# Layer 1's MLP: token operands made in every run instead of kept in DRAM, and the norm's scale row in one piece

## The chip, the cores and the metric

The kernel runs on one core of a Trainium2 chip. The metric is the device time of one execution in microseconds (us). TensorE (PE, with its weight loads as PEld), VectorE (DVE), ScalarE (ACT), GpSimd (POOL) and SyncE (SP) each work through a queue of their own in order; DMAs are issued from the queues of SP and POOL. Three runs of the kernel before took 2901.81 to 2903.02 us, with a median of 2902.23 us.

## What is computed

One inference step of a two-layer decoder: 1024 prompt tokens and 8 sampled tokens go through gated linear attention, an MLP, differential attention with a paged cache, and a second MLP, each followed by a post-norm. The part at issue is the last one, the MLP of layer 1:

```python
def post_norm(x, f, g, b):
    return layer_norm(DEEPNORM_ALPHA * x + f, g, b)

def sq_relu_mlp(x, w1, w2):
    h = jax.nn.relu(x @ w1)
    return (h * h) @ w2
...
        x_p = post_norm(x_p, f_p, ln_mix_g[layer], ln_mix_b[layer])
        x_s = post_norm(x_s, f_s, ln_mix_g[layer], ln_mix_b[layer])
        x_p = post_norm(x_p, sq_relu_mlp(x_p, mlp_w1[layer], mlp_w2[layer]), ln_mlp_g[layer], ln_mlp_b[layer])
```

`w1` is 1024 x 4096, `w2` 4096 x 1024, everything float32.

## The kernel before

Each float32 product is made of three matmuls (`mm3`, lines 185 to 188): each operand is split into a rounded part `hi` (an ACT cast, L182 for tokens, L1415 for weights) and the rest `lo` (a subtraction: on DVE for tokens, L183, on POOL for weights, L1416), and PE adds hi·hi, hi·lo and lo·hi.

The MLP of layer 1 (`mlp1`) goes through the 4096 hidden columns in four groups, called g = 0 to 3 here; the change's title calls them runs. In each group it makes the hidden values from the tokens ("up") and multiplies them with `w2` ("down"). Both halves use a seven-product scheme for a 2 x 2 block matrix product in place of eight products. The tables `UP_W`, `UP_X`, `DOWN_H`, `DOWN_W` list for each product which quarters its two operands are made of; an operand with two terms is a difference or a sum of quarters, and "run" means that it goes on from the running quarter of the product before. For the tokens the running quarter is the tile `RX`, for the weights `RW`, and for the down results `RP` (128 x 4 x 512).

The up order is 1, 2, 5, 6, 4, 3, 7. An up product has 8 output tiles of 128 x 258 with 12 matmuls each; a down product has 4 output tiles of 128 x 512 with 12 matmuls each. Results are added on DVE into the hidden tile `HF` (L1458, L1459, or ACT copies L1461, L1465) or into the residual `Y` (L1489), and relu and square follow on ACT (L1447, L1448).

The tokens' operands are made by `chip_operand` into two buffers that take turns (XH.0 and XH.1; the profile names both XH, the queue rows XH_83 and XH_84). A buffer is free when the product before the current one has ended, so an operand is made while one product runs. For a two-term operand it does, for each of two halves: a DVE subtraction of two quarters (L1388, into `RX`), an ACT cast (L182) and a DVE subtraction (L183). For the up products this is done only in group 0. Then POOL's queue stores the two parts to the DRAM tile `xc` (L1393), and in groups 1 to 3 it loads them back (L1378, two loads of 1032 KB for each product) in place of making them. Down operands are made anew in every group. The source of the up operands, `xr(0)` and `xr(1)` (profile: XR), is not read again after group 0, so the last norm's two rows are loaded into it early (L1536).

Weight quarters are loaded on SP's queue (L1412); the second term of a sum is added by a DMA on POOL's queue (L1414). 

Post-norm needs the residual times ALPHA times the row `ln_mix_g`, plus ALPHA times the row `ln_mix_b`. `alpha_row` (lines 960 to 973) does this in four column pieces of 256: a DMA on SP's queue broadcasts a piece of the row into the tile `ht` (L965), and two DVE instructions of 128 x 4 x 256 apply it to tokens 0 to 3 and 4 to 7 (L970 for the scale, L972 for the shift). `ht` has one buffer (HTB = 1), so the next piece's DMA waits on SP's queue for the second DVE instruction of the piece before.

A scheduler that simulates the program sets each queue's order at build time, within the dependencies. `tc.issue_after` adds an order without a wait.

Of the kernel before, what the change touches and what calls it, by code (L numbers as in the profile page):

```python
# [12 lines left out]
F32R = mybir.dt.float32r  # L13
# [3 lines left out]
ALU = mybir.AluOpType  # L17
# [4 lines left out]
P = 128  # L22
D = 1024
# [8 lines left out]
ALPHA = 4.0 ** 0.25  # L32
# [72 lines left out]
UP_X = {1: [(0, 0)], 2: [(1, 0)], 5: [(0, 1), (0, 0)], 6: [(1, 1), "run"], 4: [(1, 0), "run"], 3: [(1, 1)], 7: [(0, 1), (1, 1)]}  # L105
# [5 lines left out]
def hybrid_step(ctx, tc, A, dbg=None, upto=9):  # L111
    nc = tc.nc
    V, S, G, TE = nc.vector, nc.scalar, nc.gpsimd, nc.tensor
    dma = nc.sync.dma_start
# [11 lines left out]
    def mmt():  # L126
        return mm.tile([P, 512], F32, name="mmt")

    def axt():
        return ax.tile([P, 512], F32, name="axt")  # L130
# [10 lines left out]
    dr = ctx.enter_context(tc.tile_pool(name="dr", bufs=1, space=DRAM))  # L141
# [9 lines left out]
    TH = 512 + NS // 2  # L151
# [3 lines left out]
    Yt = Y.rearrange("p (t n) -> p t n", n=D)  # L155
# [399 lines left out]
    for half in range(2):  # L555
        ps = smt()
        for k in range(NB):
            t = sload(w1[k * P : (k + 1) * P, half * 2048 : (half + 1) * 2048])
# [15 lines left out]
    for k in range(NB):  # L574
        t = sload(wd[k * P : (k + 1) * P, 0:2048])
# [13 lines left out]
    tmp = s2()[:, :128].rearrange("p (n d) -> p n d", d=16)  # L589
# [21 lines left out]
    for h in range(GH):  # L611
# [7 lines left out]
        for c in range(2):  # L619
# [4 lines left out]
            for i in range(4):  # L624
                a = slice(i * P, (i + 1) * P)
# [14 lines left out]
            for li, s in enumerate(LEVELS):  # L640
# [7 lines left out]
                for i in range(4):  # L648
                    for x in xs_:
                        y = 64 if s == 64 else x + TS  # L650
# [18 lines left out]
            for i in range(4):  # L669
                a = slice(i * P, (i + 1) * P)  # L670
# [5 lines left out]
            for i in range(4):  # L676
                a = slice(i * P, (i + 1) * P)
# [7 lines left out]
                t = 4 * c + i  # L685
# [8 lines left out]
    for h in range(GH):  # L694
        hi, lo = kunit(wi, 2048 + h * 256)
# [220 lines left out]
    steps_v, steps_g = [], []  # L916
# [43 lines left out]
    def alpha_row(v, op):  # L960

        for j in range(4):
            hs = slice(256 * j, 256 * j + 256)
            r = ht.tile([P, 256], F32, name="ht")
            dma(r, v[:, hs].broadcast_to([P, 256]))  # L965
            for t in (0, 4):
                y = Yt[:, t : t + 4, hs]
                rb = bc(r, [P, 4, 256], 1)
                if op == ALU.mult:
                    steps_v.append(V.scalar_tensor_tensor(y, y, ALPHA, rb, ALU.mult, ALU.mult).ins)  # L970
                else:
                    V.scalar_tensor_tensor(y, rb, ALPHA, y, ALU.mult, ALU.add)  # L972
            yield j
# [75 lines left out]
    for u in range(12):  # L1049
        hi, lo = kunit(wd, u * 256)  # L1050
        hv, lv = (x.rearrange("p (k n) -> p k n", n=256) for x in (hi, lo))
        for t2_ in range(4):
            ps = mmt()
            for i in range(2):
                t = 2 * t2_ + i
                a = slice(t * P, (t + 1) * P)
# [6 lines left out]
            if u < 8:  # L1063
                tmp = qt.tile([P, 2, 4, 16], F32, name="qr")
# [161 lines left out]
    for h in range(8):  # L1226
        head = nxt
        for n, t in enumerate((3, 2, 1, 0, 7, 6, 5, 4) if h == 7 else (7, 1, 5, 3, 6, 0, 4, 2)):
# [4 lines left out]
            at = t % 4 if h == 7 else t // 2  # L1233
# [34 lines left out]

    RP = hp.tile([P, 4, 512], F32, name="RP")

    XR = []

    def xr(c):
        if c == len(XR):
            XR.append(cp.tile([P, NB, TH], F32, name="XR%d" % c, tag="XL%d" % c))
        return XR[c]

# [88 lines left out]
    count = [0, 0]  # L1366
    loads = []

    def chip_operand(terms, quarter, n, tmp, kept=None):


        buf = XH.t[count[0] % 2].rearrange("p k n -> p (k n)")
        count[0] += 1
        parts = [buf[:, i * 4 * TH : i * 4 * TH + 4 * n] for i in range(2)]
        hi, lo = (x.rearrange("p (k n) -> p k n", n=n) for x in parts)
        if kept and kept[1]:
            for i in range(2):
                nc.gpsimd.dma_start(parts[i], kept[0][:, i])  # L1378
            return hi, lo
        rv, tv = (x[:, : 4 * n].rearrange("p (k n) -> p k n", n=n) for x in (RX, tmp))  # L1380
        for j in (0, 2):
            b = slice(j, j + 2)
            x = quarter(*terms[0])[:, b]
            if len(terms) > 1:

                y = rv[:, b] if terms[1] == "run" else quarter(*terms[1])[:, b]
                out = (tv if terms[1] != "run" else rv)[:, b]
                V.tensor_tensor(out, x, y, op=ALU.subtract)  # L1388
                x = out
            split(hi[:, b], lo[:, b], x)  # L1390
        if kept:
            for i in range(2):
                nc.gpsimd.dma_start(kept[0][:, i], parts[i])  # L1393
        return hi, lo

    def weight_operand(terms, quarter, side=None):
# [26 lines left out]

    w1, w2 = A["mlp_w1"][1], A["mlp_w2"][1]

    xc = dr.tile([7, P, 2, 4 * TH], F32R, name="xc")

    def operands(g, up, i):
        if up:
            left = weight_operand(UP_W[i], lambda h, k: (w1, 512 * k, 1024 * g + 512 * h))  # L1430
            right = chip_operand(UP_X[i], lambda k, c: xr(c)[:, 4 * k : 4 * k + 4, :], TH, RX, (xc[i - 1], g > 0))
            return left, right

        def beside(k, t):
            r, u = beside.quarter
            TE.matmul(acc[u][k * TS : (k + 1) * TS, :], hs[:, 4 * r + k, :], t, start=g == 0 and i in (1, 3), stop=g == 3 and r == 1)


        beside.quarter = ({1: (0, 0), 3: (1, 1), 7: (0, 1), 2: (1, 0)} if g < 3 else {1: (0, 0), 5: (0, 1), 6: (1, 0), 7: (1, 1)}).get(i)
        left = chip_operand(DOWN_H[i], lambda c, k: HF[:, 4 * k : 4 * k + 4, c, :512], 512, XF[0][:, : 4 * TH] if g == 3 and i == 7 else RX)  # L1440
        right = weight_operand(DOWN_W[i], lambda k, u: (w2, 1024 * g + 512 * k, 512 * u), beside if beside.quarter else None)
        return left, right
# [8 lines left out]
    def up_tile(g, i, m, c, left, right, ps):  # L1451
        (ah, al), (bh, bl) = left, right
        ps = ps[:, :CH]
        ms, cs = slice(m * P, (m + 1) * P), slice(c * CH, (c + 1) * CH)
        for k in range(4):
            mm3(ps, ah[:, k, ms], al[:, k, ms], bh[:, k, cs], bl[:, k, cs], k == 0, k == 3)
        c11, c12, c21, c22 = (HF[:, 4 * h + m, x, cs] for h in range(2) for x in range(2))
        add = lambda out, x, y: V.tensor_tensor(out, x, y, op=ALU.add)  # L1458
        less = lambda out, x, y: V.tensor_tensor(out, x, y, op=ALU.subtract)  # L1459
        if i == 1:  # L1460
            S.copy(c12, ps)  # L1461
        elif i == 2:
            add(c11, c12, ps)
        elif i == 5:
            S.copy(c22, ps)  # L1465
        elif i == 6:
            less(c21, ps, c12)
            add(c22, c22, c21)
        elif i == 4:
            add(c21, c21, ps)  # L1470
        elif i == 3:
            less(c12, ps, c22)
        else:
            add(c22, c22, ps)
            add(c21, c21, ps)
        if c:
            for h, x in {2: [(0, 0)], 3: [(0, 1)], 7: [(1, 1), (1, 0)]}.get(i, ()):
                hidden(h, x, m)
# [23 lines left out]
    def mlp1():  # L1502
        seq = []
        for g in range(4):
            seq += [(g, 1, i) for i in (1, 2, 5, 6, 4, 3, 7)]
            seq += [(g, 0, i) for i in ((1, 5, 6, 3, 7, 4, 2) if g < 3 else (1, 5, 6, 7, 4, 3, 2))]
        nxt = operands(*seq[0])
        n = 0
        for at, (g, up, i) in enumerate(seq):
            now = nxt  # L1510
            if not up and i == 1:
                if g == 0:
                    with tc.issue_after(steps_v[-1]):
                        list(alpha_row(A["ln_mix_g"][1:2], ALU.mult))
                    beta = alpha_row(A["ln_mix_b"][1:2], ALU.add)
                else:
                    for _ in range(2):
                        next(beta, None)
            for t in range(4):
                if t == 2 and at + 1 < len(seq):  # L1520
                    nxt = operands(*seq[at + 1])
                if up:
                    for c in range(2):
                        n += 1
                        up_tile(g, i, t, c, *now, axt() if n % 2 else mmt())
                    continue
                n += 1
                down_tile(g, i, t, *now, axt() if n % 2 else mmt())
                if g == 3:
                    for c, u in {7: [(1, 1)], 4: [(1, 0)], 3: [(0, 1)], 2: [(0, 0)]}.get(i, ()):  # L1530
                        yield 4 * c + t, u
            if g == 3 and not up and i == 7:
                samples_out()
            if g == 3 and up and i == 7:
                for x, nm in ((fg, "g"), (fb, "b")):
                    dma(x, A["ln_mlp_" + nm][1:2].broadcast_to([P, D]))  # L1536
                with tc.issue_after(loads[-1]):
                    for t0, t1 in ((0, 2), (4, 8)):
                        dma(A["y_prompt"][0, t0 * P : t1 * P], A["ln_mlp_b"][1:2].broadcast_to([(t1 - t0) * P, D]))
                spare.extend(XF[0][:, 4 * TH + 512 * j : 4 * TH + 512 * (j + 1)] for j in range(4))  # L1540
# [31 lines left out]
```

## Time and profile before

| | |
|---|---|
| median of three runs | 2902.23 us |
| the profiled execution's own time | 2897.76 us |
| its span in the profile | 2896.0 us |
| mean granted PE clock | 0.981 |
| MLP of layer 1, first up matmul to last down matmul | 2169.87 to 2877.17 us |
| DMA queue of SP: bytes | 520.66 MB |
| DMA queue of POOL: bytes | 112.50 MB |
| the DRAM tile `xc`: stores, loads | 14 and 42, 1032 KB each |

The busy share of an engine is a mean over stages. PE's matmuls overlap, so its busy time hides short gaps; waits are read from the list of waits, and a slower clock from the granted clock of a window. In the list of waits a row names the waiting engine and line, what ended the wait, the total in us, the count and the longest. In a window row the columns are the window, its length, and for PE, PEld, DVE, ACT and POOL the busy us and the number of instructions, then the granted PE clock, the DMA engines' busy share and GB/s.

### The profile page before, as it was taken

The page shows a single profiled execution, that of the slowest core. Times are in us where ns is not written, and L with a number is a line of the kernel's source. Part 1 is how long each engine was busy: PE and PEld are TensorE (multiplying, and loading weights), DVE is VectorE, ACT ScalarE, POOL GpSimd, SP SyncE. Part 2 cuts the span into 40 slices and gives each one's busy share as a digit, 9 for nine tenths or more (in the row PEclk, how much of TensorE's full clock was granted, in tenths as well). Part 3 has the DMA queues.
Part 4 walks back from the last instruction along what each step waited for, and adds up shares of the span by engine and source line. Part 5 has one row for each costly group of instructions (what it writes and reads, how often), then busy time and mean ns, then how long its engine had stood idle before and what let it go on. Part 6 is the DMA issues. An engine that isn't in the chain of part 4 may idle for free. (4 is left out here: it accounts for less than half of the span.)

```text
span 2896.0 us, 52075 instructions
## 1 busy us (share of the span) xinstructions
PE 2773.3 (96%) x19653; PEld 2267.4 (78%) x19653; DVE 1882.9 (65%) x2982; ACT 1043.5 (36%) x2075; POOL 1132.4 (39%) x867
## 2 busy tenths in 40 slices
PE   8889999999999999999999999989998999999997
PEld 5666767997777777777798988888988888797985
DVE  2565544567878777778768822888538846738378
ACT  3233444252221221221231112777424535345352
POOL 1231212234333433333333321122426766777664
PEclk9899999999999999999999998999999999999998
DMA  7557651624798898898668995463447678695894
GB/s 250 181 176 261 245 177 39 231 73 145 268 350 299 301 351 303 321 323 310 254 225 302 363 341 142 101 137 82 120 132 220 174 220 222 160 287 119 258 240 88
DMA packets 285366, 636.46 MB, mean 220 GB/s; under 512 B 25510, under 2 KB 141292, under 8 KB 273852
## 3 DMA queue, kind: packets, MB, share of 16 engines
q1 hardware_dynamic: 252716, 520.66, 52.4%
q0 software_dynamic: 32400, 112.50, 16.2%
q8 instruction: 154, 2.52, 0.4%
q14 instruction: 96, 0.79, 0.1%
HBM read 575.55 MB, written 44.06 MB: 214 GB/s over the span
## 5 line engine op out<-in xcount | busy, mean ns | idle before, releaser
L174 POOL TENSOR_TENSOR wlo<-raw,whi 128x512 fp32r<-128x512 f32 x256 | 357.1, 1408 | 730.1 <-ACT whi L173 635.8
L186 PE MATMUL mmt<-whi,XH 128*128 128x256 f32 (+1 forms) x1760 | 526.1, 300 | 2.2 <-ACT Y L310 2.0
L187 PE MATMUL mmt<-wlo,XH 128*128 128x256 f32 (+1 forms) x1760 | 525.9, 299 | 0.9 <-POOL wlo L174 0.9
L186 PE MATMUL mmt<-XH,whi 128*128 128x512 f32 (+1 forms) x1216 | 436.5, 360 | 7.0 <-DVE HL L183 6.6
L188 PE MATMUL mmt<-whi,XL 128*128 128x256 f32 x1536 | 436.6, 285 | 0.5 <-DVE XL L183 0.5
L188 PE MATMUL mmt<-XH,wlo 128*128 128x512 f32 (+1 forms) x1216 | 434.3, 358 | 0.0
L173 ACT CAST whi<-raw 128x512 fp32r<-128x512 f32 x256 | 153.1, 619 | 579.5 <-PE mmt L188 206.3
L187 PEld LDWEIGHTS mmt<-wlo,XH 128*128 128x128 f32 x1760 | 332.2, 189 | 30.9 <-issue 19.0
L186 PEld LDWEIGHTS mmt<-whi,XH 128*128 128x128 f32 x1760 | 331.5, 189 | 28.2 <-issue 13.5
L790 DVE TENSOR_REDUCE sc<-pg 128x16 f32<-128x1024 f32 x256 | 309.5, 1214 | 62.5 <-POOL pg L789 59.3
L187 PE MATMUL mmt<-XL,whi 128*128 128x512 f32 x768 | 307.3, 400 | 0.0
L188 PEld LDWEIGHTS mmt<-whi,XL 128*128 128x128 f32 x1536 | 289.8, 189 | 13.5 <-issue 11.8
L789 DVE TENSOR_TENSOR pg<-pg,qb 128x1024 f32<-128x1024 f32 x192 | 263.7, 1375 | 53.4 <-DMA pg<-in_cache_k 38.2
L789 POOL TENSOR_TENSOR pg<-pg,qb 128x1024 f32<-128x1024 f32 x64 | 158.8, 2482 | 297.9 <-DMA pg<-in_cache_k 182.4
L186 PEld LDWEIGHTS mmt<-XH,whi 128*128 128x128 f32 x1216 | 230.6, 190 | 54.8 <-issue 14.6
L188 PEld LDWEIGHTS mmt<-XH,wlo 128*128 128x128 f32 x1216 | 231.0, 190 | 38.1 <-issue 5.9
L187 PE MATMUL mmt<-wlo,HH 128*128 128x512 f32 x512 | 204.7, 400 | 0.0
L188 PE MATMUL mmt<-whi,HL 128*128 128x512 f32 x512 | 204.6, 400 | 0.0
L186 PE MATMUL mmt<-whi,HH 128*128 128x512 f32 x512 | 204.4, 399 | 0.0
L187 PEld LDWEIGHTS mmt<-XL,whi 128*128 128x128 f32 x768 | 145.5, 190 | 38.3 <-issue 7.1
L1416 POOL TENSOR_TENSOR wlo<-RW,whi 128x512 fp32r<-128x512 f32 x96 | 156.7, 1762 | 37.1 <-ACT whi L1415 37.1
L1416 POOL TENSOR_TENSOR wlo<-rw,whi 128x512 fp32r<-128x512 f32 x92 | 148.8, 1690 | 43.3 <-ACT whi L1415 43.2
(441 smaller groups left out, 5745.6 us busy)
## 6 DMA issues: line engine op xcount, KB each, us to landing
pg<-in_cache_k SPq DMA_DIRECT2D x256, 512.0 KB
pg<-in_cache_v SPq DMA_DIRECT2D x256, 512.0 KB
XH<-xc POOLq DMA_DIRECT2D x42, 1032.0 KB, 8.7
raw<-in_mlp_w SPq DMA_DIRECT2D x164, 256.0 KB
swt<-in_mlp_w SPq DMA_DIRECT2D x32, 1024.0 KB
rw<-in_mlp_w SPq DMA_DIRECT2D x116, 256.0 KB
RW<-in_mlp_w POOLq DMA_DIRECT2D x96, 256.0 KB, 6.1
xc<-XH POOLq DMA_DIRECT2D x14, 1032.0 KB, 7.6
```

Source lines behind the costliest of these rows:

```text
L173: S.copy(hi[:, c], raw)
L174: G.tensor_tensor(lo[:, c], raw, hi[:, c].bitcast(F32), op=ALU.subtract)
L186: TE.matmul(ps, ah, bh, start=first, stop=False)
L187: TE.matmul(ps, ah, bl, start=False, stop=False)
L188: TE.matmul(ps, al, bh, start=False, stop=last)
L789: eng.tensor_tensor(pg, pg, qb, op=ALU.mult)
L790: return V.tensor_reduce(sc[:, n, :], pg.rearrange("p (h d) -> p h d", d=64), op=ALU.add, axis=AX.X).ins
L1416: G.tensor_tensor(lo[:, k, :], t, hi[:, k, :].bitcast(F32), op=ALU.subtract)
```

## The change

Three edits, in one region.

1. `chip_operand` no longer has a kept form: the stores to `xc`, the loads from it and the tile itself are gone. All seven up operands are made in every group from `xr(0)` and `xr(1)`.
2. The whole scale row `ln_mix_g` is loaded once, by one DMA of 128 x 1024, into the first two of the four 512-column slices of `RP` before the MLP begins. `RP` is first written by the down products.
3. The scale is applied by eight DVE instructions of 128 x 1024, one token tile each, written in group 0 at the odd steps of the up products 5, 6, 4 and 3, in place of the four pieces at the first down product of group 0. The shift row keeps `alpha_row`.

```diff
     RP = hp.tile([P, 4, 512], F32, name="RP")
 
+    grow = RP[:, 0:2, :].rearrange("p a n -> p (a n)")
+    dma(grow, A["ln_mix_g"][1:2].broadcast_to([P, D]))
+
...
-    def chip_operand(terms, quarter, n, tmp, kept=None):
+    def chip_operand(terms, quarter, n, tmp):
...
-        if kept and kept[1]:
-            for i in range(2):
-                nc.gpsimd.dma_start(parts[i], kept[0][:, i])
-            return hi, lo
...
-        if kept:
-            for i in range(2):
-                nc.gpsimd.dma_start(kept[0][:, i], parts[i])
         return hi, lo
...
-    xc = dr.tile([7, P, 2, 4 * TH], F32R, name="xc")
-
...
-            right = chip_operand(UP_X[i], lambda k, c: xr(c)[:, 4 * k : 4 * k + 4, :], TH, RX, (xc[i - 1], g > 0))
+            right = chip_operand(UP_X[i], lambda k, c: xr(c)[:, 4 * k : 4 * k + 4, :], TH, RX)
...
                 if g == 0:
-                    with tc.issue_after(steps_v[-1]):
-                        list(alpha_row(A["ln_mix_g"][1:2], ALU.mult))
                     beta = alpha_row(A["ln_mix_b"][1:2], ALU.add)
...
+                    if g == 0 and 2 <= at < 6 and t % 2:
+                        y = Yt[:, 2 * (at - 2) + t // 2, :]
+                        steps_v.append(V.scalar_tensor_tensor(y, y, ALPHA, grow, ALU.mult, ALU.mult).ins)
```

The queue orders below are those of the built programs. Line numbers of the changed kernel differ: its scale step is L1520 (before: L970), its operand difference L1387 (L1388), its additions into the hidden tile L1452 (L1458), into the residual L1483 (L1489), its weight rest L1412 (L1416), its adding DMA L1410 (L1414); L183 and L972 are the same lines in both.

DVE in group 0's up products, before: from the second pair of scale steps on (a block of four stands a few rows ahead of it).

```order
L970 SCALAR_TENSOR_TENSOR Y<-Y,ht 128x4x256 x2
L1458 TENSOR_TENSOR HF<-HF,axt 128x258
L1388 TENSOR_TENSOR RX<-XR_25083,RX 128x1032
L1458 TENSOR_TENSOR HF<-HF,axt 128x258
L183 TENSOR_TENSOR XH_84<-RX,XH_84 128x1032
L1388 TENSOR_TENSOR RX<-XR_24816,RX 128x1032
L183 TENSOR_TENSOR XH_84<-RX,XH_84 128x1032
L970 SCALAR_TENSOR_TENSOR Y<-Y,ht 128x4x256 x2
L1388 TENSOR_TENSOR RX<-XR_24816,RX 128x1032
```

The same place in the changed kernel, from the difference for product 5 to that for product 6:

```order
L1387 TENSOR_TENSOR RX<-XR_25084,XR_24817 128x1032
L1520 SCALAR_TENSOR_TENSOR Y<-Y,RP 128x1024 x3
L953 TENSOR_SCALAR XR_25084<-axt,lnp 128x512
L1520 SCALAR_TENSOR_TENSOR Y<-Y,RP 128x1024
L183 TENSOR_TENSOR XH_83<-RX,XH_83 128x1032
L1452 TENSOR_TENSOR HF<-HF,axt 128x258
L1387 TENSOR_TENSOR RX<-XR_25084,RX 128x1032
L1452 TENSOR_TENSOR HF<-HF,axt 128x258
L183 TENSOR_TENSOR XH_83<-RX,XH_83 128x1032
```

Four of the eight scale steps stand ahead of the operand of product 5; the other four stand earlier still, beside the last tiles of the attention's output product; none is left among the operands that follow.

POOL in group 0's up products, before (`xc` rows are the stores of the operands):

```order
L1393 DMA xc<-XH_83 128x2064
L1414 DMA RW<-in_mlp_w 128x512
L1416 TENSOR_TENSOR wlo<-RW,whi 128x512 x2
L1393 DMA xc<-XH_84 128x2064
L1414 DMA RW<-in_mlp_w 128x512
L1393 DMA xc<-XH_84 128x2064
L1414 DMA RW<-in_mlp_w 128x512
L1416 TENSOR_TENSOR wlo<-RW,whi 128x512
L1416 TENSOR_TENSOR wlo<-rw,whi 128x512
```

And in the changed kernel:

```order
L1410 DMA RW<-in_mlp_w 128x512 x3
L1412 TENSOR_TENSOR wlo<-RW,whi 128x512
L1410 DMA RW<-in_mlp_w 128x512
L1412 TENSOR_TENSOR wlo<-RW,whi 128x512 x3
L1410 DMA RW<-in_mlp_w 128x512 x3
```

The weights' rests no longer stand behind a store that waits for a token operand.

DVE at the turn from group 1's down products to group 2's up products, before:

```order
L972 SCALAR_TENSOR_TENSOR Y<-ht,Y 128x4x256
L1489 TENSOR_TENSOR Y<-Y,mmt 128x512
L972 SCALAR_TENSOR_TENSOR Y<-ht,Y 128x4x256 x2
L1489 TENSOR_TENSOR Y<-Y,axt 128x512
L1489 TENSOR_TENSOR Y<-Y,mmt 128x512
```

And in the changed kernel:

```order
L972 SCALAR_TENSOR_TENSOR Y<-ht,Y 128x4x256
L1483 TENSOR_TENSOR Y<-Y,mmt 128x512
L972 SCALAR_TENSOR_TENSOR Y<-ht,Y 128x4x256 x2
L1483 TENSOR_TENSOR Y<-Y,axt 128x512
L183 TENSOR_TENSOR XH_83<-XR_24817,XH_83 128x1032
L1483 TENSOR_TENSOR Y<-Y,mmt 128x512
L183 TENSOR_TENSOR XH_83<-XR_24817,XH_83 128x1032
```

Group 2's first up operand now stands on DVE right behind the last two shift steps.

## The prediction

> **What bounds the kernel now.** I read the page's head first, then windows over the stages of the MLP, then PE's waits in them, then the timeline around the longest wait.
>
> ```profile
> span 2896.0 us, 52075 instructions
> PE 2773.3 (96%) x19653; PEld 2267.4 (78%) x19653; DVE 1882.9 (65%) x2982; ACT 1043.5 (36%) x2075; POOL 1132.4 (39%) x867
> ```
>
> PE is busy 96% of the span. The change removes no matmul, so it can gain only where PE waits or runs at a lower granted clock, and lose only where PE is made to wait anew. The windows of the four up stages (g = 0 to 3) and of one down stage:
>
> ```profile
> 2169.00:2263.00 94.00, 82.13 (x643) 80.14 (x642) 75.40 (x80) 45.44 (x81) 56.89 (x53) 0.93 0.78 228
> 2359.00:2441.00 82.00, 77.59 (x640) 76.05 (x638) 35.66 (x54) 37.12 (x79) 58.22 (x55) 1.00 0.91 265
> 2530.00:2612.00 82.00, 79.69 (x646) 77.33 (x647) 29.91 (x58) 36.16 (x74) 58.50 (x57) 1.00 0.92 271
> 2701.00:2783.00 82.00, 78.99 (x637) 77.08 (x636) 29.86 (x54) 36.22 (x78) 57.57 (x54) 0.98 0.96 276
> 2262.00:2345.00 83.00, 82.53 (x393) 62.77 (x392) 71.51 (x76) 42.79 (x76) 61.50 (x44) 1.00 0.61 145
> ```
>
> The same number of matmuls takes 94 us in group 0 and 82 in the others. Group 0 has a clock of 0.93 and 12 us without PE. In groups 1 to 3, PE is idle 2.3 to 4.4 us and the DMA engines are over 0.9 busy. The down stage, in which DVE makes every operand anew and is as busy (71.5 of 83) as in group 0, loses 0.5 us. PE's waits in group 0's window, in all later ones for `xc`, and in group 0's down stage, in this order:
>
> ```profile
> PE axt L186 <- DVE HF L1459: 5.9, 2, 5.7
> PE axt L188 <- POOL wlo L1416: 2.4, 1, 2.4
> PE mmt L187 <- DVE XH L183: 2.0, 1, 2.0
> ...
>   PE axt L186: 8.9, 8
> ...
> PE smt L1436 <- ACT hs L1449: 0.5, 1, 0.5
> ```
>
> So group 0 has 10.3 us of waits with three different last causes, and groups 1 to 3 have 8.9 us in eight waits for a loaded operand. The 5.7 us wait in the timeline (DVE, POOL, PE), and the clock by slices of 10 us:
>
> ```profile
> 2210.00:2220.00 10.00, 10.00 (x85) 10.00 (x85) 9.55 (x5) 7.39 (x17) 7.68 (x9) 1.00 1.10 348
> 2220.00:2230.00 10.00, 2.71 (x15) 2.20 (x13) 9.93 (x6) 1.05 (x1) 5.30 (x6) 0.67 0.71 200
> 2230.00:2240.00 10.00, 9.17 (x54) 9.17 (x54) 8.64 (x20) 3.67 (x5) 4.72 (x5) 0.65 1.01 307
> ...
> 2214.47 0.56 POOL L1393 DMA_DIRECT2D xc<-XH  x1 [2.08 <-DVE XH L183]
> 2214.58 9.88 DVE L970 SCALAR_TENSOR_TENSOR Y<-Y,ht 128x1024 f32<-128x1024 f32 x2 [0.42 <-DMA ht<-in_ln_mix_g]
> 2215.59 1.64 POOL L1416 TENSOR_TENSOR wlo<-RW,whi 128x512 fp32r<-128x512 f32 x1
> ...
> 2221.90 1.47 POOL L1416 TENSOR_TENSOR wlo<-RW,whi 128x512 fp32r<-128x512 f32 x1
> 2230.83 0.58 PE L186 MATMUL axt<-XH,whi 128*128 128x258 f32 x1 [5.74 <-DVE HF L1459]
> ```
>
> POOL waits 2.08 us with a store of an operand at the head of its queue. Then it makes six weight rests without a pause (2215.59 to 2223.4; the first and the last are shown), and meanwhile DVE's pair of scale steps takes 9.88 us, not some 2.4. The additions that free PE's PSUM tile stand behind that pair. After the wait the granted clock is 0.65 until 2240.
>
> **The change part by part.**
>
> *Group 0.* Removed are the stores of the operands from POOL's queue, and the scale steps from among the operands.
>
> ```profile
> L1393 POOL DMA_DIRECT2D xc<-XH x14: 558/601/1213, 2158.7 to 2259.7; - x14
> L970 DVE SCALAR_TENSOR_TENSOR Y<-Y,ht 128x1024 f32<-128x1024 f32 x8 | 18.1, 2297 | 3.3 <-DMA ht<-in_ln_mix_g 3.3
> SPq L965 <- DVE Y L970: 24.6, 3, 11.2
> ```
>
> The eight scale steps stay eight, 18.1 us in all as they ran, 8 x 1.2 = 9.6 unhindered. By the order rows above, four stand with the attention's output product and four just ahead of product 5's operand, so none stands between an operand and the additions later on. The row is one DMA ahead of the MLP, which ends SP's 24.6 us behind buffers of `ht`. The slices from 2220 to 2240 hold 69 matmuls where two at the rate of 2210:2220 hold 170. The lacking 101 at 10/85 = 0.118 us are 11.9 us. Of these 8.3 are the two waits (5.9 + 2.4) and 3.6 the slow clock. I count the clock's 3.6 as gone with its wait, and of the 8.3 I keep 1.5, because the first four-step block still has 4 x 1.2 = 4.9 us to pass ahead of an operand, and the PE buffers cover only part. The 2.0 us for L183 I leave, since the change does not touch it. Term: -(8.3 - 1.5 + 3.6) = **-10.4**. Its bounds are -13.9 (all three waits and the clock) and 0 (the second rival).
>
> *Groups 1 to 3, removed.* The 42 loads and the waits for them.
>
> ```profile
> L1378 POOL DMA_DIRECT2D XH<-xc x42: 535/573/1929, 2347.2 to 2761.9; - x42
> ```
>
> They go entirely, and so does 42 x 0.57 = 24 us of issuing on POOL. Term: **-8.9**. The other loads of that stage, the weights, get engines that were over 0.9 busy freed of 43 MB; I book nothing for it.
>
> *Groups 1 to 3, added.* Per group 14 casts, 14 DVE subtractions L183 and 8 differences L1388, whose price group 0 shows (rows of its up stage; then the start of one operand):
>
> ```profile
> L182 ACT CAST XH<-RX 128x1032 fp32r<-128x1032 f32 x8 | 8.4, 1055 | 13.4 <-DVE RX L1388 7.9 <-PE mmt L188 4.9 <-PE axt L188 0.6
> L183 DVE TENSOR_TENSOR XH<-RX,XH 128x1032 fp32r<-128x1032 f32 x8 | 19.3, 2411 | 0.1
> L1388 DVE TENSOR_TENSOR RX<-XR 128x1032 f32<-128x1032 f32 x2 | 2.5, 1233 | 0.1
> ...
> 2247.51 1.06 ACT L182 CAST XH<-RX 128x1032 fp32r<-128x1032 f32 x1 [4.93 <-PE mmt L188]
> 2248.60 1.23 DVE L183 TENSOR_TENSOR XH<-RX,XH 128x1032 fp32r<-128x1032 f32 x1
> 2251.64 7.77 DVE L183 TENSOR_TENSOR XH<-RX,XH 128x1032 fp32r<-128x1032 f32 x1
> 2252.06 1.62 POOL L1416 TENSOR_TENSOR wlo<-rw,whi 128x512 fp32r<-128x512 f32 x1
> 2255.16 3.15 POOL L1416 TENSOR_TENSOR wlo<-rw,whi 128x512 fp32r<-128x512 f32 x2
> ```
>
> ACT gets 14 x 1.06 = 15 us beside its 36 to 37 of 82, DVE 22 x 1.23 = 27 beside its 30 to 36; both have room. The cost can only be lateness: an operand starts when the product before last frees its buffer and must be whole within one product (96 matmuls x 0.12 = 11.5 us). Its own work is about 1.06 + 2 x (1.23 + 1.23) = 6 us. It can be late where POOL gets between: L183 took 1.23 us alone and 7.77 while weight rests ran. As bounds I take, from below, group 0's down stage, which makes an operand a product and waits for none of them (0), and from above group 0's up stage, whose six operands made beside PE cost 2.0 us, 0.33 each, for 21 of them 7. The middle is nearer to how these stages are loaded, with DVE at 57 to 63 of 82 us and not 75 of 94. Term: **+3**.
>
> *The turn to group 2.* There the first operand's two subtractions now stand behind the last shift steps, which wait for their row (DVE, PE and POOL around the turn):
>
> ```profile
> 2527.12 2.36 DVE L972 SCALAR_TENSOR_TENSOR Y<-ht,Y 128x1024 f32<-128x1024 f32 x2 [7.19 <-DMA ht<-in_ln_mix_b]
> 2529.39 0.68 DVE L1489 TENSOR_TENSOR Y<-Y,axt 128x512 f32<-128x512 f32 x1
> 2530.18 0.36 PE L186 MATMUL axt<-XH,whi 128*128 128x258 f32 x1 [1.50 <-ACT whi L1415]
> 2531.67 1.32 POOL L1416 TENSOR_TENSOR wlo<-rw,whi 128x512 fp32r<-128x512 f32 x1
> ```
>
> DVE is through the shift at 2529.48 and the addition at 2530.07; the first half of the operand is then whole at 2531.3, the second, behind one more addition, at 2533.2. PE began at 2530.18. If nothing else interferes PE loses 1.1 us for the first half, and about 1.2 for the second. If the three rests from 2531.67 to 2535.5 get ahead of the second subtraction, it is about 6. Next in DVE's queue are the additions to `HF`, which PE needs one product later. Term: **+3**, bounds 0 (the row's DMA lands sooner, with POOL's queue empty of loads) and 6.
>
> *The rest.* The last norm's two rows are loaded into XR at the end of group 3's up stage instead of group 0; some 95 us of the last down stage cover two loads of 512 KB, and without that cover they would cost a few us. Cost 0.
>
> Sum: -10.4 - 8.9 + 3 + 3 = -13.3. The profiled execution took 2897.76 us (span 2896.0), 4.5 less than the median; the sum is a difference, so I put it to the median: 2902.2 - 13.3 = **2889**. In the profiled execution's terms that is 2884.5. The own range of this case is 2878 (-13.9 and -8.9, with +0 and +0, is -22.8, or 2879.4) to 2896 (group 0 gives half, -5.2, and the added work 7 and the turn 1: -6.1).
>
> On the slow clock: the trace shows 0.67 and 0.65 behind a wait of 5.7 us and 1.00 behind the waits of a microsecond at the turns. [...]
>
> **The rivals.**
>
> *First, slower: the lock between POOL's and DVE's two-input instructions makes the added operands late.* The place is each up product of groups 1 to 3. The operand from 2247.51 was whole at 2259.4: 11.9 us against the 11.5 of a product. If POOL meets the operand so in most of the 21 products and delays carry on through the two buffers, each costs 1 to 2 us. The removed waits (10.4 + 8.9 = 19.3 us) are used up at 19.3/21 = 0.9 us each. At 2 us: 2902.2 - 19.3 + 42 = 2925; at 1.3 us 2910. For it: 7.77 us is no rare value, since L183's mean is 2411 ns. Against it: group 0 has the same products with scale steps and additions besides and lost 2.0 us for L183, and the down stages lost nothing. [...]
>
> *Second, no change: group 0's stall stays.* It is POOL's run of six rests that holds whatever DVE instruction meets it; with the scale steps gone, a difference or L183 meets it, and the additions are as late. Then group 0 gives nothing: 2902.2 - 8.9 + 6 = 2899. For it: L183 alone took 7.77 us at 2251.64. Against: the run built up behind a store that waited 2.08 us, and those stores are gone.
>
> *Third, hidden anyway: the weights are next.* In groups 1 to 3 the adding DMAs of the weights stand behind the same engines and land just after `xc`; half of the 8.9 stays, and group 0 is paced by them too, half of 10.4: 2902.2 - 9.7 + 0 to 3 = 2893 to 2896. For it: the engines at 0.91 to 0.96, and a first matmul at 2530.18 that waited for a weight's cast. Against: 43 MB less.
>
> That the change does not do what it says is excluded by the order rows: no `xc` row is left.
>
> **How the numbers follow.** The forecast has 0.54, the first rival 0.20, the second 0.14, the third 0.09, the rest 0.03. This kernel's measurement tells 0.2% (5.8 us) from no change: faster is under 2896.4, slower over 2908.0. Faster: 0.53 of the forecast, 0.07 of the third, 0.03 of the first at its mild end: 0.63. Within: 0.01 of the forecast, 0.11 of the second, 0.02 of the third, 0.03 of the first: 0.17. Slower: 0.14 of the first, 0.03 of the second, and the rest: 0.20. The range goes from 2878, the forecast's low end, to 2909, over the second and third rivals and the first up to 1.3 us an operand.
>
> **What would show it.** In the changed kernel's profile no row of `xc`. Group 0's up stage some 10 us shorter, at a granted clock of 1.00, and the scale steps near 1.2 us each: if a wait of 5 us for `HF` remains, the second rival is right. PE's waits for DVE's `XH` in groups 1 to 3 about 3 us: over 15 in the three stages, and the first rival is right. 1 to 6 us at the turn to group 2. Waits for `rw` or `whi` in place of those for `xc` show the third. The prediction is wrong as a whole if the up stages of groups 1 to 3 take longer than the 82 us windows in which they now end.

## The result, and the profile after

Five runs of the changed kernel took 2877.55 to 2890.8 us, median 2883.61, beside 2901.81 for five runs of the kernel before. The ratio is 0.994 with a 95% interval of 0.9926 to 0.9954: 13 to 21 us faster. The forecast was 2889 in a range of 2878 to 2909. The profiled execution has a span of 2881.2 us (2896.0 before).

The windows of the four up stages and of group 0's down stage, with the bounds of the windows shown before:

```profile
2169.00:2263.00 94.00, 88.75 (x723) 87.60 (x722) 76.57 (x96) 52.06 (x90) 65.36 (x47) 0.98 0.47 102
2359.00:2441.00 82.00, 80.65 (x655) 78.02 (x654) 63.21 (x77) 47.36 (x92) 57.02 (x46) 1.00 0.56 122
2530.00:2612.00 82.00, 82.00 (x656) 79.14 (x655) 60.60 (x79) 51.48 (x100) 62.14 (x45) 1.00 0.56 117
2701.00:2783.00 82.00, 82.00 (x637) 77.23 (x636) 67.53 (x83) 53.08 (x102) 64.12 (x47) 1.00 0.74 163
2262.00:2345.00 83.00, 83.00 (x387) 62.77 (x386) 73.65 (x76) 39.37 (x69) 59.46 (x43) 1.00 0.56 127
```

DVE has gone from 30 to 36 busy us of 82 to 61 to 68, ACT from 37 to about 50, and the DMA engines from over 0.9 to 0.56 in two of three stages. PE is busy 80.65 to 82.00 of 82 us in the three up stages. Since the stages now begin and end at other times, these windows only show loads; durations are taken below from the first matmul of one stage to the first of the next.

PE's waits from the start of the MLP on, all of 0.8 us and more:

```profile
PE mmt L186 <- DVE Y L900: 2.8, 1, 2.8
PE smt L1364 <- DVE bmv L927: 2.7, 1, 2.7
PE axt L186 <- DVE HF L1453: 2.0, 1, 2.0
PE mmt L186 <- DVE HF L1453: 1.2, 1, 1.2
PE axt L186 <- DVE sz L1357: 1.1, 1, 1.1
PE axt L186 <- DVE RP L1483: 1.0, 1, 1.0
PE axt L187 <- DVE XH L183: 0.8, 1, 0.8
```

The 8.9 us for `xc` are gone, and so are the 5.7 us wait for `HF` and the wait for `rw` (2.4 us in the last down stage before). One wait for a remade operand is left, 0.8 us at the turn to group 2. There DVE waits for the shift row as before, but only 3.94 us (7.19 before):

```profile
2518.57 2.36 DVE L972 SCALAR_TENSOR_TENSOR Y<-ht,Y 128x1024 f32<-128x1024 f32 x2 [3.94 <-DMA ht<-in_ln_mix_b]
2520.85 0.68 DVE L1483 TENSOR_TENSOR Y<-Y,axt 128x512 f32<-128x512 f32 x1
2521.45 1.73 DVE L183 TENSOR_TENSOR XH<-XR,XH 128x1032 fp32r<-128x1032 f32 x1
2523.10 0.67 DVE L1483 TENSOR_TENSOR Y<-Y,mmt 128x512 f32<-128x512 f32 x1
2523.70 1.22 DVE L183 TENSOR_TENSOR XH<-XR,XH 128x1032 fp32r<-128x1032 f32 x1
...
2524.98 0.39 PE L187 MATMUL axt<-XH,whi 128*128 128x258 f32 x1 [0.76 <-DVE XH L183]
```

So the queue order did what the prediction read from it (the first subtraction behind the shift, the second behind one addition); only the row came sooner.

All kernels of the study, by their traces: group 0's up stage (first up to first down matmul), the rest of the MLP (groups 1 to 3 with group 0's down stage left out), the whole MLP, all in us; then the median time and its ratio to the kernel before, which ran beside each group of kernels with medians of 2900.79 to 2902.86 us.

| kernel | group 0 up | groups 1 to 3 | MLP | median | ratio (95% interval) |
|---|---|---|---|---|---|
| before | 104.5 | 519.1 | 707.3 | 2901.81 | 1 |
| the change | 94.5 | 505.0 | 683.2 | 2883.61 | 0.994 (0.9926 to 0.9954) |
| e8, the change again | 95.2 | 510.4 | 689.3 | 2883.55 | 0.9933 (0.9915 to 0.9952) |
| e1, scale row alone | 105.4 | 521.2 | 710.3 | 2906.4 | 1.0011 (0.9997 to 1.0024) |
| e2, remaking alone | 95.8 | 501.3 | 680.8 | 2879.17 | 0.9928 (0.9907 to 0.9949) |
| e9, remaking alone again | 95.8 | 505.1 | 684.6 | 2882.47 | 0.9932 (0.9915 to 0.9949) |
| e3, change with stores | 104.7 | 507.7 | 696.1 | 2893.06 | 0.9964 (0.9944 to 0.9984) |
| e7, stores behind rests | 103.6 | 507.6 | 694.9 | 2887.14 | 0.9946 (0.9928 to 0.9965) |
| e10, the same again | 100.4 | 502.3 | 686.4 | 2889.55 | 0.996 (0.9945 to 0.9975) |
| e6, both rows whole | 104.4 | 501.9 | 690.0 | 2885.39 | 0.9939 (0.992 to 0.9958) |
| e11, one rest twice | 94.0 | 514.0 | 691.7 | 2894.77 | 0.9981 (0.997 to 0.9993) |
| e4, both rests twice | 95.4 | 535.6 | 714.6 | 2912.44 | 1.0033 (1.0021 to 1.0046) |
| e5b, copies in groups 1 to 3 | 94.4 | 549.3 | 727.4 | 2914.43 | 1.0051 (1.0033 to 1.0068) |
| e5, copies all in group 0 | 177.0 | 506.2 | 766.9 | 2967.97 | 1.023 (1.0213 to 1.0247) |

A trace is one execution, a median is over 4 to 10. The two traces of one kernel differ by 4 to 9 us in the MLP, so a single trace settles 10 us, not 3.

### The profile page after: what moved, and what is told of

The parts are those of the page before. It is cut to its first block, busy times and chain, and to the rows that moved or that the text cites. A ratio compares the mean times of both kernels' runs of the same rounds, so it can differ in the third digit from the quotient of the medians.

```text
span 2881.2 us, 52020 instructions
## 1 busy us (share of the span) xinstructions
PE 2768.4 (96%) x19653; PEld 2265.4 (79%) x19653; DVE 1976.5 (69%) x3048; ACT 1083.6 (38%) x2117; POOL 1137.6 (39%) x811
## 5 line engine op out<-in xcount | busy, mean ns | idle before, releaser
L790 DVE TENSOR_REDUCE sc<-pg 128x16 f32<-128x1024 f32 x256 | 309.4, 1213 | 56.9 <-POOL pg L789 53.8
L789 DVE TENSOR_TENSOR pg<-pg,qb 128x1024 f32<-128x1024 f32 x192 | 261.7, 1365 | 57.2 <-DMA pg<-in_cache_k 45.4
L789 POOL TENSOR_TENSOR pg<-pg,qb 128x1024 f32<-128x1024 f32 x64 | 159.1, 2487 | 293.7 <-DMA pg<-in_cache_k 206.6
L1412 POOL TENSOR_TENSOR wlo<-rw,whi 128x512 fp32r<-128x512 f32 x92 | 160.9, 1800 | 83.9 <-ACT whi L1411 71.7
L1412 POOL TENSOR_TENSOR wlo<-RW,whi 128x512 fp32r<-128x512 f32 x96 | 169.2, 1802 | 46.8 <-ACT whi L1411 46.8
```

The source lines that it names most:

```text
L789: eng.tensor_tensor(pg, pg, qb, op=ALU.mult)
L790: return V.tensor_reduce(sc[:, n, :], pg.rearrange("p (h d) -> p h d", d=64), op=ALU.add, axis=AX.X).ins
L1412: G.tensor_tensor(lo[:, k, :], t, hi[:, k, :].bitcast(F32), op=ALU.subtract)
```

## The experiments

### The two edits apart: e1 and e2

e1 takes the kernel before and adds only the scale row and its steps:

```diff
     RP = hp.tile([P, 4, 512], F32, name="RP")
+    grow = RP[:, 0:2, :].rearrange("p a n -> p (a n)")
+    dma(grow, A["ln_mix_g"][1:2].broadcast_to([P, D]))
...
-                    with tc.issue_after(steps_v[-1]):
-                        list(alpha_row(A["ln_mix_g"][1:2], ALU.mult))
...
+                    if g == 0 and 2 <= at < 6 and t % 2:
+                        y = Yt[:, 2 * (at - 2) + t // 2, :]
+                        steps_v.append(V.scalar_tensor_tensor(y, y, ALPHA, grow, ALU.mult, ALU.mult).ins)
```

> Only the scale row is changed (one DMA, eight early steps); the operands are still stored and loaded. Measure: the MLP of layer 1 from its first up matmul to its last down matmul (707.3 us before, 683.2 after the whole change) and its group-0 up stage (104.5 before, 94.5 after). Theory A (the scale steps among the operands are what held group 0): group 0 about 95, MLP about 697, the eight waits for loaded operands stay near 9 us; time about 2892. Rival (POOL's run of rests behind a waiting store holds whatever DVE instruction meets it): group 0 stays near 104, MLP about 707, time about 2901.

Measured: group 0 at 105.4 us, no gain in time. PE waits 8.6 us for `xc`, as before. The long wait for `HF` is gone with the scale steps, and two others stand in its place, 5.8 us for `Y` at the start and 5.6 us for `wlo`. The first of them in the timeline of e1 (DVE, then POOL):

```profile
2175.12 5.28 DVE L183 TENSOR_TENSOR XH<-XR,XH 128x1032 fp32r<-128x1032 f32 x1
2180.33 0.68 DVE L900 TENSOR_TENSOR Y<-Y,mmt 128x512 f32<-128x512 f32 x1
...
2174.98 0.60 POOL L1396 DMA_DIRECT2D xc<-XH  x1
2175.60 2.49 POOL L1419 TENSOR_TENSOR wlo<-rw,whi 128x512 fp32r<-128x512 f32 x2
2178.04 1.26 POOL L1419 TENSOR_TENSOR wlo<-raw,whi 128x512 fp32r<-128x512 f32 x1
2180.70 0.57 POOL L1396 DMA_DIRECT2D xc<-XH  x1 [1.40 <-DVE XH L183]
```

Behind the store POOL makes three rests on end; L183 meets them and takes 5.28 us, not 1.23; the addition that frees PE stands behind it. So another DVE instruction is held here as the scale steps were in the kernel before, although this store did not wait. Not all of the 5.8 us is the stores' work: the change, which has none, waits 2.8 us for `Y` at this place. Theory A, by which moving the scale steps brings group 0 to about 95 us, falls.

e2 takes the change and puts the scale back into four pieces:

```diff
-    grow = RP[:, 0:2, :].rearrange("p a n -> p (a n)")
-    dma(grow, A["ln_mix_g"][1:2].broadcast_to([P, D]))
...
+                    with tc.issue_after(steps_v[-1]):
+                        list(alpha_row(A["ln_mix_g"][1:2], ALU.mult))
...
```

> Only the operands are changed (made anew in each group, nothing stored or loaded); the scale keeps its four pieces in one buffer. Theory A: group 0's up stage keeps a wait of 5 us for HF behind a pair of scale steps, about 103 us, groups 1 to 3 as in the whole change: MLP about 692, time about 2893. Rival (the stores cause the stall): group 0 about 95, MLP about 683, time about 2884.

Measured: group 0 at 95.8 us and the whole gain, 0.9928. In e2 the last pair of scale steps still stands among the operands and still takes 5.22 us, but what PE loses behind it is 2.85 us and not 5.7 (DVE, then PE):

```profile
2214.99 5.22 DVE L970 SCALAR_TENSOR_TENSOR Y<-Y,ht 128x1024 f32<-128x1024 f32 x2 [0.16 <-DMA ht<-in_ln_mix_g]
...
2222.56 0.48 PE L187 MATMUL axt<-XH,whi 128*128 128x258 f32 x1 [2.85 <-DVE XH L183]
```

What the change gains, it gains by removing the operands' stores and loads.

### The stores alone: e3, e7 and e10

e3 keeps group 0's stores in the changed kernel; nothing reads them.

```diff
+        if kept is not None:
+            for i in range(2):
+                nc.gpsimd.dma_start(kept[:, i], parts[i])
         return hi, lo
...
```

> The whole change, but group 0 still stores its 14 operand parts to DRAM from POOL's queue; nothing reads them. Theory A: group 0 about 95 to 97, MLP 683 to 686, time about 2885. Rival (stores at the head of POOL's queue make it run six rests on end): group 0 about 104, MLP about 693, time about 2894.

Measured: 104.7 us, with the two long waits of e1 at their full length:

```profile
PE mmt L186 <- DVE Y L900: 5.8, 1, 5.8
PE axt L188 <- POOL wlo L1415: 5.6, 1, 5.6
```

So the stores alone make the difference in group 0: 10 us in the traces, and 9 us in the medians (2893.06 against 2883.61 and, in e8, 2883.55 us, taken at other times; the intervals of the ratios still overlap a little). The removed loads are the other half: e1 and e3 both have stores and the new scale steps, and differ by 1.0011 against 0.9964, and by 521.2 against 507.7 us behind group 0's up stage.

e7 moves each pair of stores behind the rests of its product:

```diff
+            if g == 0:
+                with tc.issue_after(rests[-1]):
+                    for j in range(2):
+                        nc.gpsimd.dma_start(xc[i - 1][:, j], right[j].rearrange("p k n -> p (k n)"))
```

> As e3_stores_kept (the whole change, with the 14 stores of group 0 kept and read by nothing), but each pair of stores stands in POOL's queue behind the four weight rests of its own product, not between or ahead of them. The bytes and the issues are the same as in e3, whose group-0 up stage took 104.7 us. Theory B (a store at the head of POOL's queue waits for a token operand, the weight rests behind it come late and then in a row, and lock DVE out): group 0 back to 95 to 98, MLP 683 to 688, time about 2884. Rival (the stores' traffic or their issue time on POOL costs the 10 us): group 0 about 104, MLP about 695, time about 2893.

Its profiled execution took 2893.88 us, 6.7 above its median, with group 0 at 103.6 us; the median lay between the two theories. So it was run again as e10.

> e7 once more (14 stores behind the weight rests of their product), since its profiled execution was the slowest of its six. Theory B (only a store that stands ahead of rests costs): group 0 at 95 to 98 in this execution, time within 3 us of e8. Rival (the stores cost wherever they stand, by their issues on POOL and their traffic): group 0 at 102 to 105 again, time 5 to 10 us over e8.

Measured: 100.4 us, and 6 us over e8 in the medians of the same chip. PE's wait for `Y` at the start is 2.81 us, as in the change, and not 5.8: theory B holds for this stall of e1. But it is not all: stores behind the rests cost too, by another way. Of the tile `xc` in e10, who waited for it and how long its stores took; then that wait in the timeline (DVE, and PE behind it):

```profile
who waited for it (us, times):
  DVE XH L183: 5.1, 1
...
DMA to landing us min/median/max: 6.0/8.0/10.6
```

```profile
2225.49 7.38 DVE L183 TENSOR_TENSOR XH<-RX,XH 128x1032 fp32r<-128x1032 f32 x1 [5.07 <-DMA xc<-XH]
...
2234.03 0.39 PE L188 MATMUL axt<-XH,wlo 128*128 128x258 f32 x1 [3.46 <-POOL wlo L1413]
```

A store of e10 landed in the median 8.0 us after its issue, and until then it held the operand's buffer: the next operand for that buffer waits 5.07 us for it, comes just when POOL makes rests, takes 7.38 us, and PE waits for both engines. e1 (3.3 us) and e3 (2.6 us) have this wait also; the kernel before has not.

A run of rests does not need a store. e8, the change again, has one too (DVE, POOL, then PE):

```profile
2220.33 7.01 DVE L1387 TENSOR_TENSOR RX<-XR 128x1032 f32<-128x1032 f32 x1
2222.78 3.46 POOL L1412 TENSOR_TENSOR wlo<-rw,whi 128x512 fp32r<-128x512 f32 x2
2227.73 0.39 PE L186 MATMUL axt<-XH,whi 128*128 128x258 f32 x1 [2.53 <-DVE HF L1453]
```

Four rests on end, of which the last two are shown, hold a difference for 7.01 us, and PE loses 2.53. In the change's first trace POOL makes four rests on end as well (2232.45 to 2238.32), and no DVE instruction of that stage takes over 2.4 us. So it is shown that the stores cost group 0 its 10 us, but not by which step: a DVE instruction held longer, a buffer held, or traffic.

### Traffic in groups 1 to 3: e5 and e5b

Both add to the changed kernel two DRAM-to-DRAM copies for each up operand of groups 1 to 3, and two stores in group 0 that give the copies their source.

```diff
+            if g > 0:
+                for j in range(2):
+                    nc.gpsimd.dma_start(xd[i - 1][:, j], xc[:, j])
...
```

> The whole change, and for each operand of groups 1 to 3 two copies of 1032 KB from DRAM to DRAM on POOL's queue, as many issues as the removed loads and twice their bytes; no engine needs them. Theory A (only the waits for the loaded operands cost): MLP 683 to 686. Rival (their traffic and their issues also delayed the weights, which would explain why groups 1 to 3 gained 14 and not 9): groups 1 to 3 lose some 5 us, MLP about 688 or more, with waits of PE for whi, wlo or rw.

Measured: the copies, which depend on nothing late, were all put into group 0, which took 177.0 us with waits of up to 23.4 us for `wlo`. It says nothing of groups 1 to 3, only that beside this traffic and these issues on POOL's queue the weights came that late. e5b holds each pair behind its product's rests by an order on POOL's queue (`with tc.issue_after(rests[-1])`).

> The whole change, and for each up operand of groups 1 to 3 two copies of 1032 KB from DRAM to DRAM on POOL's queue, behind the weight rests of the same product, so that they lie in the stages in which the loads lay. No engine needs them. Theory B (in groups 1 to 3 only the waits for the loaded operands cost): groups 1 to 3 within 2 us of the whole change, MLP 683 to 686, time about 2884. Rival (the loads' traffic and issues also held up the weights): MLP 688 to 693, with waits of PE for whi, wlo or rw in the up stages; time about 2890.

Measured: the up stages of groups 1 to 3 took 97.8, 91.7 and 92.6 us (85.1, 84.0 and 82.8 in the change), the last down stage 102.6 (88.1), and 31 us are lost in the medians. PE's three greatest waits from the MLP's start on:

```profile
PE axt L188 <- POOL wlo L1413: 9.0, 15, 0.8
PE axt L186 <- DVE HF L1463: 8.0, 4, 2.8
PE smt L1440 <- DMA rw<-in_mlp_w: 6.7, 1, 6.7
```

The rival is right in kind: with such traffic the weights' rests come late, fifteen times. Its size is not that of the removed loads, since the copies read and write DRAM and their issues took 0.81 us in the median, those of the loads 0.57.

### What the added work costs: e4 and e11

e4 makes each token rest of groups 1 to 3 twice, e11 only that of the first half.

```diff
             split(hi[:, b], lo[:, b], x)
+            if again:
+                V.tensor_tensor(lo[:, b], x, hi[:, b], op=ALU.subtract)
...
```

> The whole change, and in groups 1 to 3 each rest of a token operand (DVE, 128x1032) is made twice, with the same result: 42 two-input instructions more, 17 to 22 us more of DVE for each up stage, which has 61 to 68 of 82 us busy. It prices the added work at its double. Theory B (the operands have cover of nearly a product's length): 0 to 6 us over the three stages, MLP 683 to 689, time 2884 to 2890. The first rival of the prediction (each added two-input instruction that meets POOL makes an operand late): 1 to 2 us for each of 21 products, MLP 704 to 725, time 2905 to 2925.

> As e4, but only one of the two rests of a token operand is made twice: 21 two-input DVE instructions more instead of 42, 9 to 11 us for each up stage. The 42 cost 31 us of MLP, 1.5 a product. If the cover ends at the edge of a product (DVE has 14 to 20 us to spare in a stage, of which the 42 took all), the 21 cost 0 to 6 us: MLP up to 689, time about 2887. If each one costs its length and more wherever it stands (no cover), half: 15 us, MLP about 698, time about 2899.

Measured in the medians against 2883.6: 28.8 us for the 42 of e4 (0.69 each), 11.2 us for the 21 of e11 (0.53 each). e11's profiled execution took 2885.09 us, 9.7 below its median, so its 691.7 us of MLP are too low for it; its median is nearer to "half" than to "covered". In e4 the up stage of group 1 holds this much:

```profile
2359.00:2441.00 82.00, 77.61 (x619) 75.39 (x619) 77.09 (x81) 41.55 (x80) 59.86 (x43) 0.98 0.51 109
```

and PE waits most for these (L1391 is the second making of a rest):

```profile
PE axt L187 <- DVE XH L1391: 14.6, 11, 6.0
PE axt L186 <- DVE HF L1455: 8.4, 8, 2.4
```

The same window in e11:

```profile
2359.00:2441.00 82.00, 80.15 (x621) 76.04 (x621) 70.06 (x86) 51.62 (x100) 60.67 (x45) 1.00 0.55 114
```

In this window DVE is at 77 of 82 us in e4 and at 70 in e11. In the windows of groups 2 and 3 it is at 74 in e4, whose stages have grown longer, and at 72 and 74 in e11. In the whole MLP of e4 PE waits eleven times for the second making of a rest. So added DVE work does make operands late, and with them the additions into `HF`, as the first rival said, and it begins soon: the change itself, at 61 to 68 us in both its traces, stands little below e11. How much of the lateness is DVE's own load and how much is POOL holding it was not separated.

### Both rows, and the change again: e6, e8 and e9

e6 treats the shift row as the scale row.

```diff
+    brow = RP[:, 2:4, :].rearrange("p a n -> p (a n)")
+    dma(brow, A["ln_mix_b"][1:2].broadcast_to([P, D]))
...
+                        V.scalar_tensor_tensor(y, brow, ALPHA, y, ALU.mult, ALU.add)
...
```

> The whole change, and the shift row ln_mix_b treated as the scale row: one DMA into the other half of RP ahead of the MLP, and eight steps of 128x1024 behind the scale steps in group 0, none at the later turns. If the turn to group 2 still costs (its DVE waits 3.9 us for the row, PE 0.8 us): MLP 682, time 1 us less. If eight more steps of 1.2 us in group 0, where DVE is busy 77 of 94 us, come late: group 0 up to 100 us, MLP up to 689, time up to 2890.

Measured: both happen. The up stages of groups 1 to 3 take 82.8 us each, the least seen in any kernel here, and group 0 takes 104.4. The time is that of the change.

> The whole change once more, unaltered, for a second profiled execution and beside e9 on the same chip. If its group-0 up stage (94.5 us) is the work of the order and not of one execution, it is 94 to 97 again, MLP 681 to 686. If the first profile was a lucky one (the granted clock falls or not behind a wait of 3 us), group 0 is 100 or more. Time about 2884. The start of the MLP, 2177 us in the first profile and 2170 to 2177 in the others, tells whether the change makes it later (2177 again) or the execution does (2170 to 2174).

> e2 once more (operands made anew, the scale row in its four pieces as before). If the whole scale row brings nothing, it is within 3 us of e8: about 2881 to 2885, with a group-0 up stage of 94 to 97. If the early scale steps cost (they stand ahead of the additions that free PE at the start of group 0), it is 3 to 5 us faster than e8; if they bring something, 3 us slower or more.

Measured: group 0 at 95.2 us again, in e9 at 95.8, so these stages are the order's work. The medians of e8 and e9 differ by 1.1 us: the whole scale row brings nothing that can be told. It trades one wait for another: the change, in both traces, waits 2.8 us for `Y` at the start of group 0 and for no operand in that stage, while e2 and e9 have no such wait for `Y` and wait 4.7 and 3.5 us for `XH`. No kernel here is clearly faster than the change; remaking alone does as well with less code.

The MLP began at 2177 us in the change's first trace, 7 us later than before, which took away from its gain. In e8 it began at 2172.7, and over all traces between 2169.9 and 2179.1; two executions of one program differ by up to 4.6 us. So the late start is put down to the execution.

## Why the prediction was right, and where it was not

**Group 0, -10.4.** Measured -10.0 and -9.3 (e8). The size was right, in part by luck, and its cause half. The step "Removed are the stores ... and the scale steps" counted both; e1 shows that the scale steps' move alone gives nothing, e2 that it isn't needed, e3 that the stores are the whole of it. PE's waits above 0.15 us in this stage fall from 12.3 us to 5.2 and 5.8 in the two traces, which leaves 2.9 and 2.8 us for the clock (0.93 before, 0.98 after) and shorter gaps; the sum had 6.8 and 3.6. But it kept 1.5 us, where 2.0 and 2.5 for `HF` stayed and a new 2.8 for `Y` came, and it left 2.0 us for L183, which went, as did some 1.5 us of small waits. These errors nearly cancel.

The second rival named a mechanism that the traces show, a run of rests that holds the DVE instruction that meets it: 5.28 us in e1, 7.01 in e8. Its outcome did not come, but the reason set against it, that the run built up behind a store, does not hold: in e8 there is such a run and no store. What is shown is that, without the stores, PE's longest wait for `HF` in this stage is 2.0 and 2.5 us and not 5.7.

**Groups 1 to 3, removed, -8.9, and added, +3 and +3.** Predicted together -2.9; the rows of the table give 505.0 - 519.1 = -14.1 and, in e8, -8.7. With e2 and e9, whose groups 1 to 3 have the same work, the mean of four traces is 505.5, or -13.6. This is the mis-sized term, and the removed part of it: the list of waits puts 8.9 us down to `xc`, and the stages lost more. An up stage in which PE has no wait above 0.15 us takes 82.8 us. The kernel before's took 88.0, 86.6 and 87.8 (the prediction's windows of 82 us are shorter than these stages), which is 13.9 us more, and its three down stages were 3.6 us longer than in the mean of the four traces, with a wait of 2.4 us for `rw` and one of 1.5 for a weight's cast at the turn. So some 17.5 us were there to be removed, not 8.9. The four traces keep 3.9 us over 82.8 in their up stages in the mean (0.7 to 8.2), where the added work and the turn were forecast at 6.

Of the 13.9 us, 8.9 are the waits for `xc`; of the rest, some is the clock, 0.79, behind the longest wait for an operand in group 3, 2.13 us. The slice of 8 us in which that wait ends, in the kernel before:

```profile
2724.00:2732.00 8.00, 7.09 (x46) 7.12 (x47) 0.00 (x0) 4.38 (x10) 5.03 (x5) 0.79 1.11 308
```

It holds 46 matmuls where a full slice holds 69. "I book nothing for it", of the engines freed of 43 MB, was the step that fell short. In every trace without the loads group 1's down stage takes 82.5 us, in the two with them 84.2 and 84.1. In e5b, beside the copies' traffic, PE waited fifteen times for the weights' rests, 9.0 us in all; what share of the 17.5 us traffic had, beside the clock, stays open.

**The added work.** Of the predicted +3, the traces show 2.0 us of PE's waits for DVE from group 1's up stage to group 3's in the change, 0.76 of them at the turn, and in e8 2.3, beside 3.3 for POOL's rests. By the stages' length it is 3.5 us in the change and 8.2 in e8, the turn included. The size held in the mean of the four traces, not in each. That there was "room" on both engines did not hold as a reason: e11 adds half as much of DVE's rests again and pays 0.53 us for each.

**The turn, +3.** PE waited 0.76 us there, and the 1.50 us that it waited before for a weight's cast are gone. It came out near the bound of 0, for the reason given there, a row that lands sooner.

**The first rival** did not come at its price, but what it describes is there: in e8 four differences (L1387) of groups 1 and 2 took 6.5 to 7.4 us, not 1.23, and those are the two stages that lost the 8.2 us. e4, with more DVE work, reaches the price that was worked out: 28.8/21 = 1.4 us for each product, and slower than before.

**The rest, 0.** In the traces without loads or copies the last instruction ends 20.2 to 20.9 us after the last down matmul begins, before and in e1 18.8 and 18.4. These 2 us are not explained; the DVE work at the end takes as long as before.

The medians moved by 18.2 us (17.2 in e8's), the MLP by 24.1 and 18.0 in the two traces; the tail's 2 us and the scatter of an execution lie between. The forecast gain was 5 us too small, by the terms of groups 1 to 3.

## What to carry to other kernels

When an operand is kept in DRAM to save an engine's work, its price is not only the waits that name the load: here the store also stood in POOL's queue ahead of other work and held its buffer until it landed (8.0 us in the median in e10), so look in the stage that writes, too. Remaking was cheap here, and this ended well before DVE was full: at 61 to 68 of 82 us it went well, one more rest for each operand (70 of 82 in group 1) cost 11 us and two (77 of 82) cost 29. And where two edits come together, undo each by itself: here one of them brought nothing that could be told.

## What the runs showed of the hardware

A wait of the same length cost the clock in one execution and not in another. In e7 and e10, the same program, PE waits 2.81 us for `Y` at the start of group 0. It ends at 2182.2 us in e7 and at 2184.9 in e10. The clock of two slices in e7, then of three in e10:

```profile
2180.00:2185.00 5.00, 2.79 (x13) 2.79 (x14) 4.97 (x9) 2.90 (x4) 5.00 (x4) 0.63 0.68 223
2185.00:2190.00 5.00, 5.00 (x32) 5.00 (x31) 0.18 (x1) 0.75 (x2) 3.77 (x6) 0.68 0.86 318
```

```profile
2180.00:2185.00 5.00, 2.19 (x19) 1.99 (x17) 4.39 (x6) 3.30 (x5) 4.77 (x3) 1.00 1.03 376
2185.00:2190.00 5.00, 5.00 (x43) 5.00 (x43) 2.88 (x6) 1.80 (x5) 4.99 (x7) 1.00 0.56 169
2187.00:2192.00 5.00, 5.00 (x44) 5.00 (x43) 1.70 (x4) 1.24 (x3) 4.49 (x6) 1.00 0.85 300
```

Behind the wait one execution runs 32 matmuls in 5 us at 0.68, the other 43 and 44 at 1.00. Beside the 2.81 us of e7, the wait of 2.13 us in group 3 of the kernel before had a lower clock behind it, 0.79. What decides it was not shown.

Two-input DVE instructions were held by several POOL instructions in a row, not one: 5.28 us (e1), 7.01 (e8), 7.38 (e10), 7.77 and, for a pair, 9.88 (both in the kernel before) were seen, where one alone took 1.23. In the attention of the kernel before, where POOL takes every fourth of the multiplications L789, those on DVE, with two inputs of 128x1024, took 1.16 to 3.14 us, and DVE's reductions L790, with one such input, 1.17 to 1.22. What decides between an instruction held so long and a run of rests that lets DVE in between, as in the change from 2232.45 on, was not found.
